# Attention outputs of heads 0 to 5: split into high and low parts at the store instead of at the reload

## The chip, the cores and the metric

The kernel runs on one core of one Trainium2 chip. The metric is the device time of one execution in microseconds. The core has five engines with a queue each, which wait for each other through semaphores: TensorE (PE in the rows, with its weight loads as PEld), VectorE (DVE), ScalarE (ACT), GpSimd (POOL) and SyncE (SP), which issues nearly all DMAs here. A queue is worked in order: an instruction that waits holds up all that stand behind it.

## The reference

One layer of a hybrid model over 1024 latent and 128 context tokens, width 1024: a half-step FFN, a token mixer, another half-step FFN, a final norm. The change lies in the mixer's attention and in the handing of its output to the up-projection:

```python
def mla_attention(q_nope, q_rope, k_nope, k_rope, v):   # 8 heads, dense softmax
    s = einsum('bqhd,bkhd->bhqk', qn, k_nope) + einsum('bqhr,bkr->bhqk', qr, k_rope)
    p = softmax(s * QK_SCALE)
    return einsum('bhqk,bkhd->bqhd', p, v)
...
merged = sigmoid(ga) * (o_attn @ w_up_attn) + sigmoid(gr) * (o_rec @ w_up_rec)
out = merged @ w_out
```

Latent queries attend to the 1024 latent keys and to 128 cached context keys; the context's 128 queries attend to the context alone.

## The kernel before

Everything is float32, and large matmuls are made of three: each operand is split into a high part (a cast to float32r, as TensorE takes it) and a low part (the operand less its high part), and high x high, high x low and low x high are summed in PSUM. So each operand of a large matmul costs a cast and a subtraction somewhere, on ScalarE, VectorE or GpSimd.

The stages follow each other: first FFN, the recurrent branch, attention (`attn`, `heads`), the merge of both branches (`merge`), second FFN. Activations lie with the features on the 128 partitions and the 1152 tokens (1024 latent, 128 context) along the row.

`heads` goes through the eight heads h, each in two blocks j of 512 queries; below, (h,j) is such a block. In `block`, nine steps over 128 keys each (t = 0 to 8) make the scores (three matmuls `sps`, L1620 to L1622), the exponential (ScalarE, `e`, L1624), its high part (ScalarE, `ehl`, L1627) and low part (GpSimd, or VectorE where t % 3 is 2, L1629). Two steps later `av` multiplies them with the values (three matmuls `po`, L1596 to L1598). Beside these steps, and woven between them, run:
- `rowmax` for a block to come: per block 12 matmuls `mps` (L1579), each followed by VectorE's maximum `mx` (L1580). They share two PSUM buffers with the projections, so TensorE can't run ahead of VectorE by more than two.
- in j = 0 of heads 1 to 6, `queries` of the next head: nine matmuls `qps` for each third of the tokens, and VectorE's subtraction and rotary products (L1560 to L1564);
- in j = 1, `keys` or `values` of the next pair of heads (heads 0 to 5), and `head_ctx`, the context queries of this head (output `pc`).
- in heads 6 and 7, `preload`, which fetches what the merge needs.

After the last step of a block, within the next block, `av` forms 1/sum on ScalarE (`rc`, L1604 and L1605) and the output `ob` (64 features x 512 queries) by three VectorE instructions (L1606 to L1608), and hands it to `put_oat`. A pair of heads makes one tile of 128 features, k = h // 2. For heads 0 to 5, `put_oat` stores the output as it is in DRAM (`oat`, one float32 array for each of the tiles 0 to 2), through SP. Heads 6 and 7 are split at once into the SBUF tiles `oh` and `ol` (L1472, L1473).

`preload` allocates `oh` and `ol` for seven tiles: 4 to 7 are the recurrent branch's, already stored in DRAM in two parts and loaded so (L1434); for 0 to 2 it loads a third of a row at a time into `oraw` (two buffers, L1440) and makes the high and low part on VectorE (L1441, L1443). Then it loads three tiles of up-projection weights and splits them (L1449, L1451). `heads` takes one step of `preload` after each step of a block, nine in a block, and a `yield` marks a step.

The order of each engine's queue is set by the framework's scheduler from the order of the code and its own estimates of durations; some instructions are pinned, none of those here. SP's queue holds stores, weight loads and `preload`'s loads in one row.

Of the kernel before, what the change touches and what calls it, by code (L numbers as in the profile page):

```python
# [9 lines left out]
F32 = mybir.dt.float32  # L10
F32R = mybir.dt.float32r
# [8 lines left out]
P = 128  # L20
D = 1024
KT = D // P
TL = 1024
TC = 128
T = TL + TC
TW = T + 8
CW = 384
NCH = T // CW
# [65 lines left out]
class Trunk:  # L94
# [630 lines left out]
    def mixer(self):  # L725
        nc, tc = self.nc, self.tc
        dram = lambda n, sh: self.dp.tile(sh, F32, name=n)
        self.sg = dram("sgates", [2, KT, P, T])
        self.orec = dram("orec", [4, 2, P, T])
        self.oat = dram("oat", [4, P, T])  # L730
        self.ahead = dram("ahead", [KT, P, REC[1] - REC[0]])
        self.wrec = dram("wrec", [KT // 2, 2, P, KT * P])
        with ExitStack() as st:
            self.fp = st.enter_context(tc.tile_pool(name="hp", bufs=1, reuse_waits="tile"))
            self.pp = st.enter_context(tc.tile_pool(name="pp", bufs=1, space=PSUM, reuse_waits="tile"))
            self.st, self.nt, self.hfb = ("sm", 3), ("t", 3), 2
            self.hgrn()
        with ExitStack() as st:
            self.kp = self.fp = st.enter_context(tc.tile_pool(name="kp", bufs=1, reuse_waits="tile"))
            self.pp = st.enter_context(tc.tile_pool(name="pp", bufs=1, space=PSUM, reuse_waits="tile"))  # L740
            self.attn()
# [686 lines left out]
    def preload(self):  # L1428
        nc = self.nc
        for k in (4, 5, 6, 7, 0, 1, 2):  # L1430
            th, tl = self.mo[k] = self.tt(F32R, "oh"), self.tt(F32R, "ol")
            if k > 3:
                for v, t in enumerate((th, tl)):
                    nc.sync.dma_start(t[:, :T].bitcast(F32), self.orec[k - 4, v])  # L1434
                yield
                continue
            for c in range(NCH):
                cs = slice(c * CW, (c + 1) * CW)
                raw = self.fp.tile([P, CW], F32, tag="vt", bufs=2, name="oraw")
                nc.sync.dma_start(raw, self.oat[k][:, cs])  # L1440
                nc.vector.tensor_copy(th[:, cs], raw)  # L1441
                yield
                nc.vector.tensor_sub(tl[:, cs], raw, th[:, cs])  # L1443
                yield
        self.ups = []
        for m in range(3):
            wh, wl, raw = self.load_up_all(m)
            self.ups.append((wh, wl))
            nc.scalar.copy(wh[:, :4], raw)  # L1449
            yield  # L1450
            nc.vector.tensor_sub(wl[:, :4], raw, wh[:, :4])  # L1451
            yield
# [8 lines left out]
            pin(nc.sync.dma_start(w[:, 4:8].rearrange("p k m -> p (k m)").bitcast(F32), src))  # L1461
        return wh, wl, raw

    def put_oat(self, h, r, cs, ob):
        nc = self.nc
        if h < 6:
            nc.sync.dma_start(self.oat[h // 2][r, cs], ob)
            return
        if self.mo[3] is None:
            self.mo[3] = self.tt(F32R, "oh"), self.tt(F32R, "ol")  # L1470
        th, tl = self.mo[3]
        nc.scalar.copy(th[r, cs], ob)  # L1472
        nc.vector.tensor_sub(tl[r, cs], ob, th[r, cs])  # L1473
# [116 lines left out]
    def av(self):  # L1590
        nc = self.nc
        h, j, t, po, V, eh, el = self.pend.pop(0)
        o = h % 2
        v = V[t // 3][:, t % 3].rearrange("p a d -> p (a d)")
# [11 lines left out]
        nc.vector.scalar_tensor_tensor(ob[A], po[B], -1.0, r[A], ALU.mult, ALU.mult)  # L1606
        nc.vector.tensor_mul(r[A], po[A], r[A])
        nc.vector.scalar_tensor_tensor(ob[A], ob[A], 2.0, r[A], ALU.add, ALU.mult)  # L1608
        self.put_oat(h, A, ts(j, 512), ob[A])

    def block(self, h, j, q, kt, V):
        nc = self.nc
# [22 lines left out]
    def head_ctx(self, h, qc, ktc, Vc):  # L1635
# [17 lines left out]
        po = self.pp.tile([64, P], F32, tag="tr", bufs=1, name="poc")  # L1653
        nc.tensor.matmul(po, Vc[:, r], Pt, start=True, stop=True)
        nc.scalar.copy(Pt[r], po)
        self.put_oat(h, r, slice(TL, T), Pt[r])
        yield

    def half(self, name, dt=F32):
# [823 lines left out]
```

## Time and profile before

| | us |
|---|---|
| three runs, median | 2806.1 |
| lowest and highest | 2804.52, 2806.98 |
| the profiled execution's own time | 2806.0 |
| its span, first to last instruction | 2804.2 |

The page gives busy time by engine. A busy TensorE is not TensorE at its peak, because matmuls overlap: one of 512 columns is shown with 0.39 us, and the next starts 0.23 us later. So holes are read better from the weight loads' idle time, with what ended it in brackets behind the row. Windows are stretches of the span; for each engine they give the busy time and, in parentheses, the number of its instructions, and at the end the granted TensorE clock, the DMA engines' busy share and GB/s. Attention's blocks lie between about 1540 and 1850 us of the span, and the granted clock is 1.00 in all of them.

### The profile page before, as it was taken

What the parts mean: (1) busy time and instruction counts of PE and PEld (TensorE: products, weight loads), DVE (VectorE), ACT (ScalarE), POOL (GpSimd) and SP (SyncE); (2) the same over time, 40 slices, a digit from 0 to 9 for tenths busy, and PEclk for the clock granted to TensorE, in tenths of its full rate; (3) what the DMA queues carried; (4) which work ended last, traced back from release to release, by engine and by line L of the source; (5) the groups of instructions that cost most, each with busy time, mean ns of one, the idle gap of its engine ahead of it and who ended that gap; (6) DMA issues with size and microseconds to landing.
All of it is one profiled execution on the core that took longest, in us unless ns stands there. A gap on an engine that the chain in (4) does not pass through costs nothing. (4 is left out here: it accounts for less than half of the span.)

```text
span 2804.2 us, 55762 instructions
## 1 busy us (share of the span) xinstructions
PE 2755.3 (98%) x21248; PEld 2633.2 (94%) x21248; DVE 2043.0 (73%) x4461; ACT 1299.5 (46%) x2695; POOL 922.9 (33%) x983
## 2 busy tenths in 40 slices
PE   9999999999999999999999999999999999999998
PEld 8999999999999998899998888689999999999997
DVE  8877777677778888887456777867666765568875
ACT  6532322322166677666436777741642322334332
POOL 0133223454221222222233444431414343423451
PEclk9999999999999999999999999999999999999999
DMA  6743333653121111212513001263454444357521
GB/s 260 228 132 120 124 127 125 242 203 110 58 94 59 44 61 41 66 45 85 187 63 102 19 14 29 86 242 122 144 174 132 156 141 137 113 170 249 163 85 68
DMA packets 219579, 337.66 MB, mean 120 GB/s; under 512 B 23664, under 2 KB 141360, under 8 KB 219312
## 3 DMA queue, kind: packets, MB, share of 16 engines
q1 hardware_dynamic: 218880, 333.96, 36.1%
q8 instruction: 168, 2.75, 0.4%
q14 instruction: 99, 0.81, 0.1%
q10 hardware_dynamic: 432, 0.14, 0.0%
HBM read 248.47 MB, written 85.54 MB: 119 GB/s over the span
## 5 line engine op out<-in xcount | busy, mean ns | idle before, releaser
L1933 PE MATMUL b<-xo,wo 128*128 128x288 f32 x3552 | 483.7, 295 | 1.1 <-DVE wo L1908 1.1
L1933 PEld LDWEIGHTS b<-xo,wo 128*128 128x128 f32 x3552 | 475.4, 188 | 1.3 <-DVE wo L1908 1.3
L1933 PE MATMUL b<-bh,wo 128*128 128x288 f32 x1776 | 366.2, 295 | 0.2 <-DVE hf L1866 0.2
L551 PE MATMUL mm<-xh,wh 128*128 128x384 f32 x928 | 323.7, 349 | 4.4 <-DVE sg L863 3.0
L553 PE MATMUL mm<-xh,wl 128*128 128x384 f32 x928 | 313.8, 338 | 0.0
L552 PE MATMUL mm<-xl,wh 128*128 128x384 f32 x928 | 313.1, 337 | 0.0
L1933 PEld LDWEIGHTS b<-bh,wo 128*128 128x128 f32 x1776 | 288.8, 188 | 0.4 <-ACT wo L1907 0.4
L581 DVE SCALAR_TENSOR_TENSOR x<-dn,modt,x 128x256 f32<-128x256 f32 (+4 forms) x472 | 225.4, 499 | 82.0 <-PE dn L553 79.8
L1933 PE MATMUL b<-bl,wo 128*128 128x288 f32 x888 | 261.9, 295 | 0.0
L1907 ACT CAST wo<-raw 128x512 fp32r<-128x512 f32 x185 | 114.7, 621 | 221.6 <-issue 90.4
L1908 DVE TENSOR_TENSOR wo<-raw,wo 128x512 fp32r<-128x512 f32 x185 | 127.6, 691 | 80.5 <-ACT wo L1907 78.0
L2134 PE MATMUL d<-xd,wd 128*128 128x288 f32 x1344 | 181.2, 296 | 5.0 <-DVE x L2121 3.5
L2134 PEld LDWEIGHTS d<-xd,wd 128*128 128x128 f32 x1344 | 178.5, 188 | 7.5 <-DVE x L2121 3.2
L551 PEld LDWEIGHTS mm<-xh,wh 128*128 128x128 f32 x928 | 174.7, 188 | 11.0 <-DVE sg L863 3.4
L552 PEld LDWEIGHTS mm<-xl,wh 128*128 128x128 f32 x928 | 175.0, 189 | 0.9
L553 PEld LDWEIGHTS mm<-xh,wl 128*128 128x128 f32 x928 | 174.9, 188 | 0.0
L1629 POOL TENSOR_TENSOR ehl<-e,ehl 128x512 fp32r<-128x512 f32 x93 | 122.0, 1315 | 150.9 <-ACT ehl L1627 78.2
L405 DVE SCALAR_TENSOR_TENSOR junk<-wada,cb 128x512 bf16<-128x512 f32 x224 | 164.1, 733 | 7.5 <-DMA wada<-in_w_aT 6.7
L1933 PEld LDWEIGHTS b<-bl,wo 128*128 128x128 f32 x888 | 167.4, 189 | 0.0
L1903 POOL TENSOR_TENSOR ws<-raw 128x256 f32<-128x256 f32 x74 | 66.0, 912 | 277.4 <-DMA raw<-in_w 200.2
L551 PE MATMUL ps<-bh,wh 128*128 128x288 f32 (+1 forms) x448 | 135.7, 303 | 1.3 <-DVE sl L1855 1.1
L1908 DVE TENSOR_TENSOR wo<-ws,wo 128x512 fp32r<-128x512 f32 x74 | 69.8, 943 | 87.7 <-ACT wo L1907 87.4
(478 smaller groups left out, 7172.1 us busy)
## 6 DMA issues: line engine op xcount, KB each, us to landing
raw<-in_w SPq DMA_DIRECT2D x148, 256.0 KB, 3.3
wada<-in_w_aT SPq DMA_DIRECT2D x112, 256.0 KB, 2.9
raw<-in_w SPq DMA_DIRECT2D x42, 512.0 KB, 4.1
raw<-in_w_in SPq DMA_DIRECT2D x41, 512.0 KB, 3.6
xr<-xd SPq DMA_DIRECT2D x56, 288.0 KB, 4.1
hr<-hs SPq DMA_DIRECT2D x26, 576.0 KB, 5.7
hb<-hd SPq DMA_DIRECT2D x44, 288.0 KB, 3.9
hs<-et SPq DMA_DIRECT2D x84, 144.0 KB, 2.3
```

Source lines behind the costliest of these rows:

```text
L405: nc.vector.scalar_tensor_tensor(junk, ws[n % 2], 1.0, cs[s], ALU.mult, ALU.mult, accum_out=o)
L551: pin(nc.tensor.matmul(ps, wh, xh, start=start and i == 0, stop=False))
L552: pin(nc.tensor.matmul(ps, wh, xl, start=False, stop=False))
L553: self.last_mm = nc.tensor.matmul(ps, wl, xh, start=False, stop=stop and i == n - 1)
L581: nc.vector.scalar_tensor_tensor(self.x[m][:, a:b], ps[:, a - lo : b - lo], self.modt[:, gm, m, s : s + 1], self.x[m][:, a:b], ALU.mult, A ...
L1629: eng.tensor_sub(el, e, eh)
L1903: nc.gpsimd.tensor_tensor(o[:, c], x[:, c], y[:, c], op)
L1907: nc.scalar.copy(wh, src[i])
L1908: nc.vector.tensor_sub(wl, src[i], wh)
L1933: nc.tensor.matmul(ps, w[:, k], x[:, k, :QW], start=first, stop=last, skip_group_check=home != i)
L2134: nc.tensor.matmul(ps, w[:, k], xv, start=start, stop=stop, skip_group_check=home != i)
```

## The change

For heads 0 to 5, the split is made where the output is formed, on VectorE, and both parts are stored: `oat` becomes two arrays for each tile. `preload` then loads `oh` and `ol` for tiles 0 to 2 with one DMA each and does nothing on VectorE; the number of its steps stays the same. The high part of `ob` goes into `rc`, which is free by then, and the low part into `ob` itself; the context output `pc` gets a small tile `pch` for its high part.

```diff
@@ mixer
-        self.oat = dram("oat", [4, P, T])
+        self.oat = dram("oat", [3, 2, P, T])
@@ preload
-            for c in range(NCH):
-                cs = slice(c * CW, (c + 1) * CW)
-                raw = self.fp.tile([P, CW], F32, tag="vt", bufs=2, name="oraw")
-                nc.sync.dma_start(raw, self.oat[k][:, cs])
-                nc.vector.tensor_copy(th[:, cs], raw)
-                yield
-                nc.vector.tensor_sub(tl[:, cs], raw, th[:, cs])
-                yield
+            for v, t in enumerate((th, tl)):
+                nc.sync.dma_start(t[:, :T].bitcast(F32), self.oat[k, v])
+                for _ in range(3):
+                    yield
@@ put_oat
-    def put_oat(self, h, r, cs, ob):
+    def put_oat(self, h, r, cs, ob, hi):
         nc = self.nc
         if h < 6:
-            nc.sync.dma_start(self.oat[h // 2][r, cs], ob)
+            nc.vector.tensor_copy(hi, ob)
+            lo = ob.bitcast(F32R)
+            nc.vector.tensor_sub(lo, ob, hi)
+            for v, t in enumerate((hi, lo)):
+                nc.sync.dma_start(self.oat[h // 2, v][r, cs], t.bitcast(F32))
             return
@@ av
-        self.put_oat(h, A, ts(j, 512), ob[A])
+        self.put_oat(h, A, ts(j, 512), ob[A], r[A].bitcast(F32R))
@@ head_ctx
-        self.put_oat(h, r, slice(TL, T), Pt[r])
+        hi = self.fp.tile([P, P], F32R, tag="pch", bufs=1, name="pch")
+        self.put_oat(h, r, slice(TL, T), Pt[r], hi[r])
```

The scheduler orders every queue anew from it. Outside attention the order of TensorE's matmuls stays as it was. Three places matter later. Each row below is a line of the code, an instruction, its output and inputs, and the output's size; line numbers of the changed kernel differ by up to four around `preload` and are the same from L1470 to L1655.

First, VectorE in block (6,1), from the store of the first output of head 6 on. Before:

```order
L1473 TENSOR_TENSOR ol<-ob,oh 64x512
L1441 CAST oh<-oraw 128x384
L1580 TENSOR_REDUCE mx_21306<-mps 128x1
L1443 TENSOR_TENSOR ol<-oraw,oh 128x384
L1580 TENSOR_REDUCE mx_21306<-mps 128x1 x3
L1441 CAST oh<-oraw 128x384
L1583 TENSOR_REDUCE m_21424<-mx_21306 128x4
L1629 TENSOR_TENSOR ehl<-e,ehl 128x512
L1443 TENSOR_TENSOR ol<-oraw,oh 128x384
L1441 CAST oh<-oraw 128x384
L1443 TENSOR_TENSOR ol<-oraw,oh 128x384
L1629 TENSOR_TENSOR ehl<-e,ehl 128x512
```

And of the changed kernel:

```order
L1473 TENSOR_TENSOR ol<-ob,oh 64x512
L1580 TENSOR_REDUCE mx_21357<-mps 128x1 x4
L1629 TENSOR_TENSOR ehl<-e,ehl 128x512
L1583 TENSOR_REDUCE m_21468<-mx_21357 128x4
L1629 TENSOR_TENSOR ehl<-e,ehl 128x512
```

The casts and subtractions of `oraw` are gone from between the row maxima and the exponentials' low parts.

Second, VectorE in block (2,0), behind the output of (1,1), whose last instruction is the first row. Before:

```order
L1608 SCALAR_TENSOR_TENSOR ob<-ob,rc 64x512
L1560 TENSOR_TENSOR ql_17932<-qps,qh_17931 64x256
L1562 TENSOR_TENSOR u<-qps,rope 32x256
L1563 TENSOR_TENSOR u<-qps,rope 32x256
L1580 TENSOR_REDUCE mx_19245<-mps 128x1
L1564 TENSOR_TENSOR u<-u 32x256
L1580 TENSOR_REDUCE mx_19245<-mps 128x1 x2
```

And of the changed kernel:

```order
L1608 SCALAR_TENSOR_TENSOR ob<-ob,rc 64x512
L1560 TENSOR_TENSOR ql_17932<-qps,qh_17931 64x256
L1463 CAST rc<-ob 64x512
L1562 TENSOR_TENSOR u<-qps,rope 32x256
L1465 TENSOR_TENSOR ob<-ob,rc 64x512
L1563 TENSOR_TENSOR u<-qps,rope 32x256
L1580 TENSOR_REDUCE mx_19262<-mps 128x1
L1564 TENSOR_TENSOR u<-u 32x256
L1580 TENSOR_REDUCE mx_19262<-mps 128x1 x2
```

The cast and the subtraction of the new split (L1463, L1465) stand ahead of three row maxima.

At the same place TensorE's queue, up to the first matmul of the second third of the query projection (`qps`). Before:

```order
L1598 MATMUL po<-ehl,V 128x512
L1620 MATMUL sps<-qh_17929,kth_17818 128x512
L1579 MATMUL mps<-kth_17818,qh_17929 128x384 x2
L1621 MATMUL sps<-qh_17929,ktl_17819 128x512
L1622 MATMUL sps<-ql_17930,kth_17818 128x512
L1596 MATMUL po<-ehl,V 128x512
L551 MATMUL qps<-qnh_17489,wh 128x384
```

And of the changed kernel:

```order
L1598 MATMUL po<-ehl,V 128x512
L1620 MATMUL sps<-qh_17929,kth_17818 128x512
L1621 MATMUL sps<-qh_17929,ktl_17819 128x512
L1622 MATMUL sps<-ql_17930,kth_17818 128x512
L1596 MATMUL po<-ehl,V 128x512
L1579 MATMUL mps<-kth_17818,qh_17929 128x384
L1597 MATMUL po<-ehl,V 128x512
L1579 MATMUL mps<-kth_17818,qh_17929 128x384
L1598 MATMUL po<-ehl,V 128x512
L1620 MATMUL sps<-qh_17929,kth_17818 128x512
L1621 MATMUL sps<-qh_17929,ktl_17819 128x512
L551 MATMUL qps<-qnh_17489,wh 128x384
```

The two `mps` moved behind three and four matmuls of 512 columns, and `qps` behind four more than before.

Third, SP's queue where `preload` begins with tile 0. Before:

```order
L1434 DMA ol<-orec 128x1152
L1440 DMA oraw<-oat 128x384 x2
L1467 DMA oat<-ob 64x512
L1440 DMA oraw<-oat 128x384 x7
L1458 DMA raw<-in_w_up 128x512
```

And of the changed kernel:

```order
L1434 DMA ol<-orec 128x1152
L1438 DMA oh<-oat 128x1152
L1467 DMA oat<-rc 64x512
L1467 DMA oat<-ob 64x512
L1438 DMA ol<-oat 128x1152
L1438 DMA oh<-oat 128x1152
L1438 DMA ol<-oat 128x1152
L1438 DMA oh<-oat 128x1152
L1438 DMA ol<-oat 128x1152
L1454 DMA raw<-in_w_up 128x512
```

Nine loads of thirds of a row became six of whole rows, and the last store of head 5 became two.

## The prediction

> **What bounds the kernel now.** I read first the shares of the whole span, then the windows of the attention blocks one by one, then TensorE's weight-load waits inside them, then what VectorE did there. The shares:
>
> ```profile
> PE 2755.3 (98%) x21248; PEld 2633.2 (94%) x21248; DVE 2043.0 (73%) x4461; ACT 1299.5 (46%) x2695; POOL 922.9 (33%) x983
> ```
>
> TensorE is the bound, so only its holes can be won or lost. The change touches the attention stage alone. A head h is worked in two blocks, j=0 and j=1; I write (h,j). I cut the stage where each block's closing logarithm (L1604) starts; the rows are, in order, (2,0), (2,1), (4,0), (6,0), (6,1), (7,0), (7,1), with window, length, and each engine's busy time:
>
> ```profile
> core 0: us, PE busy (x) PEld busy (x) DVE busy (x) ACT busy (x) POOL busy (x), PEclk, DMA share, GB/s
> ...
> 1603.80:1624.80 21.00, 20.94 (x100) 16.97 (x100) 17.46 (x33) 15.71 (x30) 11.34 (x10) 1.00 0.03 7
> 1624.80:1644.80 20.00, 19.97 (x98) 16.14 (x97) 13.94 (x29) 16.69 (x34) 8.60 (x8) 1.00 0.07 19
> ...
> 1686.50:1708.10 21.60, 21.06 (x100) 16.93 (x99) 18.35 (x33) 15.67 (x29) 10.91 (x10) 1.00 0.03 7
> ...
> 1769.80:1792.70 22.90, 20.74 (x98) 16.49 (x97) 21.02 (x37) 15.48 (x29) 11.29 (x9) 1.00 0.15 44
> 1792.70:1813.40 20.70, 16.96 (x76) 12.40 (x76) 19.35 (x32) 14.01 (x27) 9.59 (x8) 1.00 0.12 32
> 1813.40:1830.50 17.10, 16.19 (x73) 12.55 (x73) 15.25 (x25) 13.80 (x24) 7.03 (x6) 1.00 0.44 145
> 1830.50:1844.00 13.50, 12.56 (x51) 8.24 (x50) 8.83 (x15) 11.61 (x23) 2.59 (x2) 1.00 0.01 4
> ```
>
> In (2,0) to (4,0) TensorE is idle for 0.0 to 0.5 us of a block. In (6,0) and (6,1) it stands 2.2 and 3.7 us, and VectorE is busy 21.02 of 22.90 and 19.35 of 20.70: there VectorE paces. The waits of the weight loads show each hole (the bracket: idle time before it, and who ended it). First two of (2,0) and one of (4,0), then those over 0.6 us of (6,0), (6,1) and (7,0):
>
> ```profile
> 1610.37 0.47 PEld L1579 LDWEIGHTS mps<-kth,qh 96*128 96x128 f32 x2 [0.49 <-ACT qc L1557]
> 1611.69 0.19 PEld L551 LDWEIGHTS qps<-qnh,wh 128*128 128x128 f32 x1 [0.33 <-DVE mx L1580]
> ...
> 1701.80 0.30 PEld L1586 LDWEIGHTS mtr<-ident,m 128*1 128x1 f32 x4 [0.85 <-DVE m L1583]
> ...
> 1776.48 0.30 PEld L1579 LDWEIGHTS mps<-kth,qh 96*128 96x128 f32 x2 [0.90 <-DVE mx L1580]
> 1778.80 0.19 PEld L551 LDWEIGHTS qps<-qnh,wh 128*128 128x128 f32 x1 [1.21 <-DVE mx L1580]
> ...
> 1791.44 0.19 PEld L1579 LDWEIGHTS mps<-kth,qh 96*128 96x128 f32 x1 [1.08 <-DVE mx L1580]
> 1798.74 0.14 PEld L1650 LDWEIGHTS ptc<-ident,pc 128*128 128x128 f32 x1 [1.24 <-ACT oh L1472]
> 1802.05 0.19 PEld L1579 LDWEIGHTS mps<-kth,qh 96*128 96x128 f32 x1 [1.21 <-DVE mx L1580]
> 1806.21 0.19 PEld L1598 LDWEIGHTS po<-ehl,V 128*128 128x128 f32 x1 [1.08 <-DVE ehl L1629]
> 1812.71 0.19 PEld L1579 LDWEIGHTS mps<-kth,qh 96*128 96x128 f32 x1 [1.81 <-DVE mx L1580]
> 1819.68 0.19 PEld L1598 LDWEIGHTS po<-ehl,V 128*128 128x128 f32 x1 [1.10 <-DVE ehl L1629]
> 1822.00 0.19 PEld L1579 LDWEIGHTS mps<-kth,qh 96*128 96x128 f32 x1 [0.68 <-DVE mx L1580]
> ```
>
> **What goes: nine casts (L1441) and nine subtractions (L1443) in the last heads.** VectorE's own rows in (6,1), and the two groups with their count, busy time and mean:
>
> ```profile
> 1800.09 1.45 DVE L1441 CAST oh<-oraw 128x384 fp32r<-128x384 f32 x1
> ...
> 1801.92 0.54 DVE L1443 TENSOR_TENSOR ol<-oraw,oh 128x384 fp32r<-128x384 f32 x1
> ...
> 1804.12 0.35 DVE L1441 CAST oh<-oraw 128x384 fp32r<-128x384 f32 x1
> ...
> 1804.46 1.70 DVE L1629 TENSOR_TENSOR ehl<-e,ehl 128x512 fp32r<-128x512 f32 x1
> ...
> 1810.58 1.61 DVE L1443 TENSOR_TENSOR ol<-oraw,oh 128x384 fp32r<-128x384 f32 x1
> 1812.12 1.64 DVE L1580 TENSOR_REDUCE mx<-mps 128x1 f32<-128x384 f32 x3
> ```
> ```profile
> L1443 DVE TENSOR_TENSOR ol<-oraw,oh 128x384 fp32r<-128x384 f32 x9 | 8.2, 913 | 0.1
> L1441 DVE CAST oh<-oraw 128x384 fp32r<-128x384 f32 x9 | 5.2, 582 | 0.7 <-DMA oraw<-oat 0.6
> ```
>
> So 8.2 + 5.2 = 13.4 us of VectorE leave (6,0) to (7,0). What TensorE gets back:
> - (6,0) has the matmuls of (2,0) and (4,0) (98 to 100 records). Without the splits it falls to their lengths: 22.9 - 21.0 = 1.9, or 22.9 - 21.6 = 1.3. I take 1.9.
> - (6,1): the row maxima that TensorE waits for at 1802.05 and 1812.71 stand right behind the cast of 1.45 and the subtraction of 1.61 us: 1.21 + 1.81 = 3.0 go. The wait of 1.08 at 1806.21 stands behind a cast of 0.35, but also behind an exponential's own subtraction of 1.70 us; I take half. Sum 3.5, bounds 3.0 and 4.1. The 1.24 us at 1798.74 (a context probability) has no split ahead of it and stays; it is late next there.
> - (7,0): the two waits, 1.10 and 0.68, each have one split among several things ahead. 0 to 1.2; I take 0.5.
>
> Together **5.9 us gained, 4.3 to 7.2**. Where VectorE no longer paces (6,1), ScalarE with 14.0 us of work is next, and that is under the 20.7 - 3.5 = 17.2 left.
>
> **What comes: a cast and a subtraction behind each of twelve output blocks and six context outputs.** The subtraction is shown, clean, for both shapes (heads 6 and 7 are split so already):
>
> ```profile
> 1799.49 0.67 DVE L1473 TENSOR_TENSOR ol<-ob,oh 64x512 fp32r<-64x512 f32 x1
> ...
> 1809.26 0.28 DVE L1473 TENSOR_TENSOR ol<-pc,oh 64x128 fp32r<-64x128 f32 x1
> ```
>
> The row maxima of (2,0) that follow in VectorE's queue start here:
>
> ```profile
> 1610.04 0.56 DVE L1580 TENSOR_REDUCE mx<-mps 128x1 f32<-128x384 f32 x1
> ```
>
> A cast of 64x512 is not in the trace: at least 0.35 (the cast of 384 columns), at most 0.67 (the subtraction of 512); by columns 0.35 x 512/384 = 0.46, which I take. So 0.46 + 0.67 = 1.13 us per block, and 0.35 x 128/384 + 0.28 = 0.40 per context output: 12 x 1.13 + 6 x 0.40 = 16.0 us. VectorE's total work grows by 2.6 us; the change only moves it to blocks where TensorE paces. What of it TensorE feels:
> - The split of (h,0) runs in (h,1). There VectorE is busy 13.94 of 20.00, with 6 us free; I take 0.1 for each of six, bounds 0 and 0.25: 0.6.
> - The split of (h,1) runs in (h+1,0), six times, in front of the maxima at 1610.04 for which TensorE already waits. A price is in the trace: a product of 0.55 us (L1564) took 1.69 in (4,0), 1.14 more, and (4,0) is 21.6 - 21.0 = 0.6 us longer than (2,0), with a new wait of 0.85. So 0.6 is the upper end.
>
> ```profile
> 1616.53 0.55 DVE L1564 TENSOR_TENSOR u<-u 32x384 f32<-32x384 f32 x1
> ...
> 1699.27 1.69 DVE L1564 TENSOR_TENSOR u<-u 32x384 f32<-32x384 f32 x1
> ```
>
> The new order puts four more 512-column matmuls ahead of the query projection that waits there. Matmuls of that size follow each other each 0.23 us:
>
> ```profile
> 1800.19 0.39 PE L1597 MATMUL po<-ehl,V 128*128 128x512 f32 x1
> 1800.42 0.40 PE L1598 MATMUL po<-ehl,V 128*128 128x512 f32 x1
> ```
>
> So 0.93 us of other work covers 1.13: 0.2 is left, and six times that is 1.2, bounds 0 and 3.6. If this cover fails, it is the 0.6.
>
> **Transfers.** Eighteen stores become 36; SP, which issues them, does nothing else between blocks. Nine loads become six of 576 KB; five of them no longer wait for VectorE, but for buffers that the last query projection, in (6,0), frees. The issue of the up-projection weights that stands behind them on SP, the page's row of loads of that size (count, KB, us to landing), and a window in which many overlap (last number: GB/s):
>
> ```profile
> 1812.59 0.42 SPq L1458 DMA_DIRECT2D raw<-in_w_up  x1
> ```
> ```profile
> hr<-hs SPq DMA_DIRECT2D x26, 576.0 KB, 5.7
> ```
> ```profile
> 1850.00:1870.00 20.00, 20.00 (x153) 20.00 (x152) 11.21 (x26) 4.42 (x10) 8.53 (x10) 1.00 1.05 388
> ```
>
> Five loads are 2.95 MB, 7.6 us at 388 GB/s: from 1792.7, the end of (6,0), they land at 1800, and the weights behind them are issued some 20 us sooner than at 1812.59. One after the other they would take 5 x 5.7 = 29 us, to 1821: still ahead of the merge at 1844, but behind the opening of (7,0), where ScalarE now casts those weights with exponentials queued behind. I take 0, since the window shows that such loads overlap.
>
> **The sum.** -5.9 + 0.6 + 1.2 = **-4.1 us**. The profiled execution took 2806.0 us (span 2804.2), 0.1 under the median of three, 2806.1. So 2806.0 - 4.1 = **2801.9**. About 0.2%, 5.6 us, is what a measurement here can tell from no change: below 2800.5 counts as faster, above 2811.7 as slower.
>
> **Rivals.**
> - *Cover complete:* the order hides all splits, and the late heads give 5.9 to 7.2: about 2799.5. For: 6 us of free VectorE in j=1 blocks, the moved matmuls. Against: the waits that (2,0) has already.
> - *Collisions:* both new operations are of the kinds that sometimes take far longer here: L1443 means 913 ns against 540 clean, L1441 582 against 350, so 0.37 + 0.23 a block. Over twelve that is 7.2 us of VectorE; half falls in j=0 blocks, and 0.6/1.14 of that reaches TensorE: 1.9 us, so 2803.8. The 1.45 us cast at 1800.09 starts inside a GpSimd subtraction (a POOL row starts at 1799.97 and lasts 1.34), so it looks like a lock.
>
> ```profile
> 1799.97 1.34 POOL L1629 TENSOR_TENSOR ehl<-e,ehl 128x512 fp32r<-128x512 f32 x1 [1.42 <-PE sps L1622]
> ```
>
> The Trainium skill, "SBUF — State Buffer", section "Who interferes with whom", says that a cast, and a subtraction of two SBUF inputs, share ports with GpSimd and that the second to start blocks until the first is done; by that rule the trace agrees (1.45 against 0.35), and each split is exposed, which speaks against the change and for 2803.8 rather than 2801.9.
> - *Chain instead of VectorE:* in (6,1) the exponential, its cast and GpSimd's subtraction become the bound, as in (7,1), where TensorE stands 0.9 of 13.5 with VectorE at 8.83; then (6,1) and (7,0) give 1.0 instead of 4.0: -1.1, 2804.9.
> - *Slower:* the splits sit in VectorE's queue ahead of the row maxima whose two PSUM buffers TensorE needs, and all lands: 16.0 - 5.9 = +10.1, 2816.1. It loses from 0.5 us per block on (5.9/12). Against: (4,0) shows 0.6 in a j=0 block only, with no new order.
>
> **How the numbers follow.** Forecast 0.42, cover complete 0.25, collisions 0.20, chain 0.05, slower 0.08. The range reaches from the best gain with little cost (2806.0 - 7.2, and 0.9 for what runs of before differ: 2798.0) to a forecast whose costs are all at their bounds (2806.0 - 4.3 + 3.6 + 1.5 = 2806.8, 2807.0); it leaves out the slower case and the tail of the first. Faster: cover complete and a fifth of the forecast, 0.33; slower 0.08; same 0.59.
>
> **What would show it.** (6,1) near 17 us without waits of over 1 us for mx; (6,0) near 21; (1,0) to (5,0) longer by 0.2, with the wait before the second query projection still under 0.6. New L1463 and L1465 rows of over 1 us, or j=1 blocks longer than 20.0, would prove me wrong towards collisions or slower.

## The result and the profile after

| | before | after |
|---|---|---|
| time, median of 18 runs each | 2806.6 us (2804.3 to 2808.8) | 2811.3 us (2809.5 to 2813.5) |
| profiled execution, its span | 2806.0 us, 2804.2 us | 2813.5 us, 2811.4 us |

The ratio is 1.0019, 95% interval 1.0013 to 1.0026: the changed kernel is 4.7 us **slower**, where 4.1 us faster was forecast.

The shares of the whole span after the change (busy time, share, instructions of each engine):

```profile
PE 2757.1 (98%) x21248; PEld 2633.0 (94%) x21248; DVE 2053.5 (73%) x4479; ACT 1301.1 (46%) x2695; POOL 927.6 (33%) x983
```

VectorE is busy 10.5 us longer (2053.5 against 2043.0), where the working of the forecast had 2.6. The windows of single blocks after, cut as in the prediction, in order (0,1), (1,0), (1,1), (2,0), (2,1), then (6,0) to (7,1):

```profile
core 0: us, PE busy (x) PEld busy (x) DVE busy (x) ACT busy (x) POOL busy (x), PEclk, DMA share, GB/s
1542.50:1563.60 21.10, 20.23 (x98) 16.05 (x97) 16.31 (x33) 17.04 (x35) 9.15 (x7) 1.00 0.11 26
1563.60:1584.30 20.70, 20.26 (x98) 16.61 (x97) 17.71 (x33) 15.79 (x30) 12.06 (x11) 1.00 0.08 20
1584.30:1607.10 22.80, 21.75 (x107) 16.98 (x106) 15.13 (x29) 16.76 (x33) 9.25 (x8) 1.00 0.11 29
1607.10:1629.40 22.30, 20.94 (x99) 16.92 (x98) 19.40 (x35) 15.88 (x30) 11.14 (x10) 1.00 0.06 13
1629.40:1650.20 20.80, 20.45 (x99) 16.15 (x98) 15.88 (x33) 17.05 (x36) 9.90 (x8) 1.00 0.11 26
1780.50:1802.50 22.00, 20.77 (x99) 16.74 (x98) 18.90 (x34) 15.60 (x28) 10.50 (x9) 1.00 0.42 140
1802.50:1820.00 17.50, 16.49 (x77) 12.76 (x76) 12.52 (x25) 14.13 (x28) 8.02 (x7) 1.00 0.39 140
1820.00:1837.00 17.00, 15.85 (x70) 11.67 (x70) 13.14 (x21) 14.32 (x26) 8.40 (x6) 1.00 0.15 47
1837.00:1849.90 12.90, 12.48 (x52) 8.66 (x51) 8.31 (x13) 11.05 (x23) 2.80 (x3) 1.00 0.00 0
```

(6,1) fell from 20.7 to 17.5, as forecast, and (2,1), a j=1 block in which VectorE is still idle for 4.9 us, grew from 20.0 to 20.8. All lengths, to 0.01 us between the starts of the closing logarithms of two blocks, in one table; "L1465" is the duration of the new subtraction in that block:

| block | (0,1) | (1,0) | (1,1) | (2,0) | (2,1) | (3,0) | (3,1) | (4,0) | (4,1) | (5,0) | (5,1) | (6,0) | (6,1) | (7,0) | (7,1) |
|---|---|---|---|---|---|---|---|---|---|---|---|---|---|---|---|
| before | 20.01 | 20.72 | 20.92 | 21.02 | 20.01 | 20.76 | 20.93 | 21.64 | 19.99 | 20.75 | 20.92 | 22.84 | 20.79 | 17.08 | 13.51 |
| after minus before | +1.08 | 0.00 | +1.92 | +1.28 | +0.73 | -0.04 | +1.97 | +0.66 | +0.81 | -0.06 | +1.95 | -0.76 | -3.31 | -0.07 | -0.61 |
| L1465 | 1.78 | 0.68 | 1.78 | 1.33 | 1.20 | 0.68 | 1.81 | 1.33 | 1.20 | 0.68 | 1.80 | 1.41 | | | |

The last four blocks win 4.75 us, the eleven before them lose 10.30, of which the six j=1 blocks 8.46. That is +5.6, against +4.7 between the medians and +7.2 between the two profiled spans: the rest of the 7.2 lies before and behind these blocks, and the profiled execution of the changed kernel was the slowest of its 18.

The third row sorts the blocks. Where the subtraction took 0.68 us, the block kept its length, though it had 1.1 us more of VectorE; where it took 1.2 to 1.8, the block grew ((6,0) against what it should have won, as the next section shows). What happens in (1,1): VectorE's and GpSimd's rows, then TensorE's weight load that waits (start, duration, engine, line, operation, tiles):

```profile
1589.64 0.42 DVE L1463 CAST rc<-ob 64x512 fp32r<-64x512 f32 x1
1590.10 0.56 DVE L1580 TENSOR_REDUCE mx<-mps 128x1 f32<-128x384 f32 x1
1590.68 1.78 DVE L1465 TENSOR_TENSOR ob<-ob,rc 64x512 fp32r<-64x512 f32 x1
1592.50 0.56 DVE L1580 TENSOR_REDUCE mx<-mps 128x1 f32<-128x384 f32 x1
```
```profile
1590.63 1.29 POOL L1629 TENSOR_TENSOR ehl<-e,ehl 128x512 fp32r<-128x512 f32 x1 [4.53 <-ACT ehl L1627]
```
```profile
1593.11 0.19 PEld L1579 LDWEIGHTS mps<-kth,qh 96*128 96x128 f32 x1 [1.47 <-DVE mx L1580]
```

GpSimd's subtraction begins at 1590.63, VectorE's 0.05 us later. GpSimd's ends at 1591.92, VectorE's 0.54 us behind that. This holds in all nine blocks in which the subtraction is long: GpSimd's row began 0.03 to 0.90 us before it, and VectorE's ended 0.55 us after GpSimd's each time, to 0.01 us, for the 0.68 that it takes alone. So its length is what is left of GpSimd's row, and 0.55. The next row maximum stands behind it in the queue and begins at 1592.50, and TensorE, out of PSUM buffers for scores, has stood still 1.47 us. In (1,0) the order of the two is the other way round:

```profile
1568.99 0.68 DVE L1465 TENSOR_TENSOR ob<-ob,rc 64x512 fp32r<-64x512 f32 x1
1569.70 0.43 DVE L1563 TENSOR_TENSOR u<-qps,rope 32x256 f32<-32x256 f32 x1
1570.16 0.56 DVE L1580 TENSOR_REDUCE mx<-mps 128x1 f32<-128x384 f32 x1
1570.75 0.42 DVE L1564 TENSOR_TENSOR u<-u 32x256 f32<-32x256 f32 x1
```
```profile
1569.16 3.16 POOL L1629 TENSOR_TENSOR ehl<-e,ehl 128x512 fp32r<-128x512 f32 x2 [4.10 <-PE sps L1622]
```

VectorE began at 1568.99, GpSimd 0.17 later; VectorE is clean and GpSimd's two rows take 3.16 us together (a single one has a median of 1.29 in the trace of before). And the sum L1564 behind it, here a clean 0.42 us, was stretched at this place before the change:

```profile
1568.00 1.06 DVE L1564 TENSOR_TENSOR u<-u 32x256 f32<-32x256 f32 x1
```

So (1,0) paid for a part of its 1.1 us of new work with stretching that went away: 0.64 us here, 0.37 over the whole block, since a later L1564 in it is now stretched by 0.28. Blocks of one kind repeat this to 0.03 us: 1.78, 1.81, 1.80 in (1,1), (3,1), (5,1).

So the theory was: **stretching** (the "collision theory" of the expectations: the second to start of two operations with two SBUF inputs, one on VectorE and one on GpSimd, waits for the first), in front of the row maxima, whose delay TensorE then feels. Its rivals: plain **work** (1.1 us in front of the maxima costs, stretched or not), and **order** (the scheduler's new order of TensorE and ScalarE costs). In the runs below, "blocks" is the sum of (0,1) to (5,1) minus before, "late" that of (6,0) to (7,1); times and ratios are against runs of the kernel before on the same chip, with 95% intervals.

### The profile page after: what moved, and what is told of

The parts are those of the page before. It is cut to its first block, busy times and chain, and to the rows that moved or that the text cites. A ratio compares the mean times of both kernels' runs of the same rounds, so it can differ in the third digit from the quotient of the medians.

```text
span 2811.4 us, 55837 instructions
## 1 busy us (share of the span) xinstructions
PE 2757.1 (98%) x21248; PEld 2633.0 (94%) x21248; DVE 2053.5 (73%) x4479; ACT 1301.1 (46%) x2695; POOL 927.6 (33%) x983
```

## The gain alone and the cost alone

```diff
-            nc.vector.tensor_copy(hi, ob)
-            lo = ob.bitcast(F32R)
-            nc.vector.tensor_sub(lo, ob, hi)
-            for v, t in enumerate((hi, lo)):
-                nc.sync.dma_start(self.oat[h // 2, v][r, cs], t.bitcast(F32))
+            for v in range(2):
+                nc.sync.dma_start(self.oat[h // 2, v][r, cs], ob)
```

> The gain alone: heads 0 to 5 store the unsplit output twice, with no cast and no subtraction, and the last heads load the two parts as in the changed kernel; this leaves the split of heads 0 to 5 out. All theories: (0,1) to (5,1) as long as before the change, (6,0) to (7,1) shorter by about 4.7 us together as in the changed kernel, 2801.5 to 2802.5. If the late heads gain less than that here, part of the 4.7 came from elsewhere.

Measured: 2799.6 us against 2805.3, ratio 0.9980 (0.9972 to 0.9989). Late -5.83: (6,0) -1.72, (6,1) -3.42, (7,0) -0.06, (7,1) -0.63. The other blocks are within 0.03 of before, but for (4,0), -0.63, where an L1564 of 1.69 us took 0.55. The windows of (6,0) and (6,1):

```profile
1769.79:1790.91 21.12, 20.65 (x101) 16.89 (x99) 16.97 (x32) 15.45 (x29) 10.70 (x9) 1.00 0.49 166
1790.91:1808.28 17.37, 16.37 (x76) 12.64 (x75) 12.39 (x25) 14.06 (x27) 7.76 (x6) 1.00 0.35 122
```

The time is 1.9 us under what was expected. The 5.9 us of the forecast are there, and 1.1 more than the changed kernel shows, since its last split still runs in (6,0). This kernel makes all the new stores and loads, so the transfers cost nothing that shows. The split is what costs. It was then put alone into the kernel before:

```diff
 # kernel before
         if h < 6:
+            nc.vector.tensor_copy(hi, ob)
+            nc.vector.tensor_sub(hi, ob, hi)
             nc.sync.dma_start(self.oat[h // 2][r, cs], ob)
```

> The cost alone: the kernel before with the cast and the subtraction of the split added on VectorE behind each output of heads 0 to 5 (their result is stored nowhere), the unsplit output stored and the last heads loading and splitting as before. Collision theory: subtractions of over 1 us in most blocks, and 8 to 11 us more than before, 2814 to 2818; blocks where the subtraction takes 0.7 keep their length. Work theory: the same total, but blocks with a clean subtraction grow too. If it is under 2810, the transfers or the two stores of the changed kernel had a part in the cost.

Measured: 2814.9 against 2805.3, ratio 1.0036 (1.0023 to 1.0048). Blocks +9.72, of which j=1 8.40, each block within 0.07 us of the changed kernel's but for (5,0), 0.32 shorter. (1,0), (3,0) and (5,0), with a subtraction of 0.68, did not grow, as the first theory had it and the second had not. So the cost in these blocks is that of the split on VectorE, with one store or two, whatever the last heads do. (The last four blocks were 1.8 us longer than before here, (7,0) by 4.1 and (6,1) 2.3 shorter; why stays open.)

## Taking the stretching away

First the same operands in another instruction:

```diff
-            nc.vector.tensor_sub(lo, ob, hi)
+            nc.vector.scalar_tensor_tensor(lo, ob, 1.0, hi, ALU.mult, ALU.subtract)
```

> The changed kernel with one edit: the subtraction of the split (L1465) is written as scalar_tensor_tensor (ob*1.0 - hi), same operands, same result, same place in every engine's order. Collision theory (the new subtraction, 0.68 us clean, is locked out by a GpSimd subtraction in nine of twelve blocks and takes 1.20 to 1.81 us, and the row maxima behind it come late): scalar_tensor_tensor on the same two tiles (L1608) was never stretched, so L1465 takes about 0.68 in all twelve, (0,1) to (5,1) fall back towards their old lengths, and the time falls by 7.5 us (the sum of the stretching) to 10.4 us (the sum by which those blocks grew): 2801 to 2804. Work theory (1.1 us more on VectorE in front of the row maxima is what costs, stretched or not): at least half of the 10.4 stays, 2806 to 2809. Order theory (TensorE's and ScalarE's new order costs it): no change, 2811.

Measured: 2810.3, ratio 1.0018 (1.0009 to 1.0027); blocks +10.16. The time is the one named for the order theory, but the run puts no theory to the test, since the stretching was still there:

```profile
L1465 DVE SCALAR_TENSOR_TENSOR ob<-ob,rc x12: 683/1330/1801, 1549.6 to 1787.9; 64x512 fp32r<-64x512 f32 x12
```

The columns are minimum, median and maximum in ns. The expectation rested on L1608, the same kind of operation, which was never stretched in the kernel before (0.67 to 0.69 us in 16 rows). That was luck of its place, not of its kind: in the changed kernel one of its 16 rows, in (7,0), took 1.67. What has to go is the second SBUF input:

```diff
-            nc.vector.tensor_sub(lo, ob, hi)
+            nc.vector.tensor_reduce(lo[:, 0:1], hi, AX.X, ALU.max)
```

> The changed kernel with the subtraction (L1465) replaced by a row maximum over the same 64x512 high part, an operation with one SBUF input; every engine keeps the order of the changed kernel instruction by instruction. The low part is left out (it holds the unsplit output). Collision theory: no row of L1465 over 0.8 us whatever GpSimd does beside it, (0,1) to (5,1) fall from 10.4 us over their old lengths to 0 to 3, time 2801 to 2804. Work theory (any 0.7 us there costs): at least 7 of the 10.4 stay, 2808 to 2811. Order theory: all of it stays, 2811.

Measured: 2807.2 against 2807.2, ratio 0.9999 (0.9990 to 1.0008), every queue keeps the order of the changed kernel, and the row is clean in all twelve:

```profile
L1465 DVE TENSOR_REDUCE ob<-rc x12: 666/675/684, 1547.4 to 1782.3; 64x1 fp32r<-64x512 f32 x12
```

In (1,1) the pair met as in the changed kernel, GpSimd 0.04 us ahead, and where TensorE had waited 1.47 us it now waits 0.37:

```profile
1589.88 0.68 DVE L1465 TENSOR_REDUCE ob<-rc 64x1 fp32r<-64x512 f32 x1
```
```profile
1589.84 1.28 POOL L1629 TENSOR_TENSOR ehl<-e,ehl 128x512 fp32r<-128x512 f32 x1 [4.53 <-ACT ehl L1627]
```
```profile
1591.21 0.19 PEld L1579 LDWEIGHTS mps<-kth,qh 96*128 96x128 f32 x1 [0.37 <-DVE mx L1580]
```

In the j=1 blocks this is the cleanest number of the study. There L1465 was stretched by 5.49 us in the changed kernel (1.78 + 1.78 + 1.20 + 1.81 + 1.20 + 1.80 less six times 0.68), and 8.46 - 5.49 = 2.97. With no stretching and the same order, the j=1 blocks cost 2.96: there **the stretching reaches TensorE one for one**. It holds block by block, too: from (0,1) to (5,1) the growth less the stretching is -0.02, 0.82, 0.21, 0.84, 0.29 and 0.83, and this run measures -0.06, 0.81, 0.26, 0.83, 0.33 and 0.79. But all blocks together still cost 6.78, where the first theory expected 0 to 3 and 2801 to 2804 us, and the work theory 2808 to 2811: the time lies between the two. The j=0 blocks got worse, from +1.84 to +3.82: (1,0), (3,0), (5,0) went from 0 to +0.9. Here is (1,0):

```profile
1567.21 0.68 DVE L1465 TENSOR_REDUCE ob<-rc 64x1 fp32r<-64x512 f32 x1
1567.92 0.43 DVE L1563 TENSOR_TENSOR u<-qps,rope 32x256 f32<-32x256 f32 x1
1568.38 0.56 DVE L1580 TENSOR_REDUCE mx<-mps 128x1 f32<-128x384 f32 x1
1568.97 1.39 DVE L1564 TENSOR_TENSOR u<-u 32x256 f32<-32x256 f32 x1
```
```profile
1568.79 1.29 POOL L1629 TENSOR_TENSOR ehl<-e,ehl 128x512 fp32r<-128x512 f32 x1
```

Where the split had two SBUF inputs and came first, it held GpSimd back, and L1564 found GpSimd's next operation out of its way. Now GpSimd begins 0.18 us before L1564, and L1564 waits for it: 1.39 - 0.42 = 0.97 us, and the block is 0.97 longer. The stretching had moved to the next candidate. Two ways take it from the split with its full result kept (in both, and in the one on GpSimd behind them, the scheduler orders the queues anew), first by PSUM:

```diff
-        nc.vector.scalar_tensor_tensor(ob[A], ob[A], 2.0, r[A], ALU.add, ALU.mult)
+        fin = po[A] if h < 6 else ob[A]
+        nc.vector.scalar_tensor_tensor(fin, ob[A], 2.0, r[A], ALU.add, ALU.mult)
...
+        # put_oat: hi = cast of fin, lo (SBUF) = fin (PSUM) - hi
```

> The changed kernel with the last product (L1608) of heads 0 to 5 written to the PSUM tile po instead of SBUF, so that the cast and the subtraction of the split have one PSUM and one SBUF input; the result is the same. Collision theory: L1465 about 0.7 us in all twelve blocks; the cast may take 0.7 instead of 0.42 and the PSUM buffer comes free 1 us later; 2801 to 2806. Work theory: VectorE's clean work is as much or more (1.1 to 1.4 us a block), so 2809 to 2812.

Measured: 2808.4 against 2807.2, ratio 1.0003 (0.9994 to 1.0012). The j=1 blocks fell to +2.74, the j=0 blocks rose to +5.29, with L1564 stretched by 0.7 to 1.1 us in each; the cast from PSUM took 0.69. Then by ScalarE, which moves the subtraction to another time:

```diff
-            nc.vector.tensor_copy(hi, ob)
+            nc.scalar.copy(hi, ob)
...
-            nc.vector.tensor_sub(lo, ob, hi)
+            nc.vector.scalar_tensor_tensor(lo, ob, 1.0, hi, ALU.mult, ALU.subtract)
```

> The changed kernel with the cast on ScalarE and the subtraction as scalar_tensor_tensor: VectorE does 0.68 us a block instead of 1.1 clean. Collision theory: as with scalar_tensor_tensor alone, or up to 1 us better, 2800 to 2804; ScalarE has 0.45 us more in blocks where it is busy 14 to 16 of 20 us, which may cost 0 to 0.2 a block. Work theory: better than scalar_tensor_tensor alone by 2 us or more. Order theory: nothing can be said, since the order differs here.

Measured: 2805.4 against 2805.3, ratio 1.0000 (0.9991 to 1.0009). L1465 took 0.68 to 0.69 in all twelve, being the first to start each time, and the j=1 blocks cost 1.20; the j=0 blocks cost 4.02, with 1.6 to 1.85 us of stretching in the three L1564 of each. Two of them in (1,0), the smaller form first:

```profile
1568.45 1.40 DVE L1564 TENSOR_TENSOR u<-u 32x256 f32<-32x256 f32 x1
1575.78 1.29 DVE L1564 TENSOR_TENSOR u<-u 32x384 f32<-32x384 f32 x1
```

Both times were over what the first theory expected, and the stretching of L1564 is the likely reason; the first is also only 0.6 us under what the work theory had. And the subtraction on GpSimd itself:

```diff
-            nc.vector.tensor_sub(lo, ob, hi)
+            nc.gpsimd.tensor_sub(lo, ob, hi)
```

> The changed kernel with the subtraction of the split on GpSimd, the cast on VectorE; the result is the same. Collision theory: VectorE's row maxima are not held up by the split itself, but GpSimd has about 1.3 us more in front of its exponentials' low parts, and VectorE's other two-input operations meet it: cost of 0 to 6 us, 2800 to 2806. Work theory: as with the cast alone plus GpSimd's delay, 2803 to 2809.

Measured: 2816.7 against 2807.2, ratio 1.0033 (1.0021 to 1.0046), worse than any theory said. One such subtraction takes GpSimd 1.29 us, and (3,0) and (5,0) grew by 3.1 and 3.2, with one L1564 of 2.61 us in each. The engine that is the other party of the stretching is no refuge.

## The other candidate

L1564 can lose its second SBUF input too, if the second product of the rotation stays in the PSUM tile that it reads:

```diff
-                nc.vector.tensor_mul(u[R, 1], ps[96:P, v], rope[96:P, lo:hi])
-                nc.vector.tensor_add(u[R, 0], u[R, 0], u[R, 1])
+                nc.vector.tensor_mul(ps[R, v], ps[96:P, v], rope[96:P, lo:hi])
+                nc.vector.tensor_add(u[R, 0], u[R, 0], ps[R, v])
```

In the kernel before:

> The kernel before with only L1563 written to PSUM (control). Collision theory: L1564 was stretched there by 0.23 to 1.15 us in (1,0) to (5,0), and only the 1.15 of (4,0) was seen to cost 0.6: 2803.5 to 2806, and (4,0) as long as (2,0). Work or order theory: no change, 2806.5.

Measured: 2803.6 against 2805.3, ratio 0.9991 (0.9982 to 0.9999). L1564 before, and now:

```profile
L1564 DVE TENSOR_TENSOR u<-u x24: 416/550/1694, 1491.5 to 1789.1; 32x384 f32<-32x384 f32 x16, 32x256 f32<-32x256 f32 x8
```
```profile
L1564 DVE TENSOR_TENSOR u<-u,qps x24: 419/552/554, 1490.3 to 1787.1; 32x384 f32<-32x384 f32 x16, 32x256 f32<-32x256 f32 x8
```

The median is the same, the maximum is gone, and (4,0) is 0.37 us shorter, now as long as (2,0) (21.27 and 21.29), which itself grew by 0.27. The scheduler's order changed with the edit, and 1.6 of the 2.0 us that these blocks won lie in the last four, where no L1564 had been stretched: so the 1.7 us are not shown to be L1564's. The same edit beside the three ways of the split:

> The changed kernel with the row maximum in place of the subtraction (as in the run before with it, the low part is left out), and with the second product of the query rotation (L1563) written to the PSUM tile it reads, so that the sum behind it (L1564) has one SBUF input. Collision theory (each two-input operation of VectorE that meets a GpSimd one is stretched, and when the split no longer is, L1564 is: 1.24 to 1.54 us more in (1,0), (3,0), (5,0)): no L1564 row over 0.7 us, (1,0), (3,0) and (5,0) fall by 0.9 each, the even j=0 blocks by 0.2, so 3 to 4.5 us less than with L1564 as it was: 2803 to 2804.5, and what then stays of the cost in (0,1) to (5,1), 2.5 to 4 us, is the clean work of the split. Work or order theory: L1564 had no part, and the time stays at 2807.

> The changed kernel with the cast of the split on ScalarE, its subtraction as scalar_tensor_tensor, and L1563 written to PSUM; the result is the same. Collision theory: with the cast on ScalarE no split was stretched, but L1564 was by 1.6 to 1.85 us in each j=0 block, and these blocks were 0.5 to 1.1 us longer; with L1564 clean they are within 0.3 of before: 2800.5 to 2803. ScalarE theory (its 0.61 us cast holds up exponentials in j=0 blocks): no change, 2805.

> The changed kernel with the last product (L1608) of heads 0 to 5 in PSUM, and L1563 written to PSUM: neither the split nor L1564 has two SBUF inputs, all on VectorE, same result. Collision theory: j=0 blocks, 0.6 to 1.6 us longer than before with L1564 stretched by 0.7 to 1.1, fall to 0 to 0.5; 2803 to 2805.5. Work theory: no change, 2808.

Measured: 2811.1 (ratio 1.0017, 1.0009 to 1.0026), 2806.9 (1.0006, 0.9997 to 1.0016) and 2805.6 (1.0001, 0.9992 to 1.0010): two misses, and the third at the edge of what was expected. The order is another one in all three. No L1564 was stretched in any of them, and yet the eleven blocks together cost 9.67, 5.19 and 6.99 us, where they had cost 6.78, 5.21 and 8.03 without this edit. In the first the *cast* now met GpSimd:

```profile
L1463 DVE CAST rc<-ob x12: 407/424/1478, 1548.1 to 1786.1; 64x512 fp32r<-64x512 f32 x12
```

By 1.07 in (1,1) and (3,1) and by 0.63 in (2,1) and (4,1), which cost 1.7 and 1.3. In the second, the split's subtraction was again stretched by 1.02, 1.05 and 1.12 in (2,0), (4,0) and (6,0). In the third nothing of the split was, but one exponential's subtraction (L1630 there) by 1.1 in (0,1), and (5,1) was 5.0 us longer and (5,0) 2.5 shorter: work moved across the cut, which left 87 and 116 matmuls in them for 97 and 106 in the run with PSUM alone. In the first two another pair met once the queues had shifted. That the j=0 blocks pay for L1564's stretching is therefore shown where the order was kept, with the row maximum ((1,0), (3,0) and (5,0) 0.97, 0.95 and 0.95 us longer than in the changed kernel for 0.97, 0.96 and 0.96 of stretching), and not confirmed by these three.

## Work or order: what is left

```diff
-            nc.vector.tensor_sub(lo, ob, hi)
```

> The changed kernel without the subtraction: the cast alone is on VectorE and the unsplit output is stored as the low part; this leaves the low part out. Collision theory: the cast was never stretched (0.41 to 0.43), so blocks (0,1) to (5,1) cost 0 to 1.5 us together and the time is 2799.5 to 2801.5. Work theory: 0.42 of 1.1 us of work stays, so about 4 us of cost: 2803 to 2805. The order of TensorE and ScalarE is a different one here, so up to 2 us may be put down to it.

Measured: 2802.2 against 2807.2, ratio 0.9983 (0.9975 to 0.9992); blocks +1.79, of which (1,1), (3,1), (5,1) +0.54 to +0.58 each, with no cast stretched. The 2.96 us of the unstretched j=1 blocks were then cut down step by step, with the order kept in the first step:

```diff
-            nc.vector.tensor_sub(lo, ob, hi)
+            nc.vector.memset(ob.bitcast(BF16)[:, : ob.shape[-1]], 0.0)
```

> The changed kernel with the subtraction (L1465) replaced by a fill of the low part's first 256 words (the low part is left out); every engine keeps the order of the changed kernel instruction by instruction, and the fill has no SBUF input and should take about 0.27 us (a fill of 128x256 took 0.272 elsewhere in the kernel) where the row maximum took 0.68 and the subtraction 0.68 to 1.81. If what is left of the cost without stretching is clean work in VectorE's queue, the blocks that had no stretching with the row maximum fall by about the 0.41 that is taken out, (1,1), (3,1), (5,1) from +0.8 to +0.4 and (2,1), (4,1) from +0.3 to 0, 2.5 to 4 us less than with the row maximum in sum: 2802.5 to 2805. If it is the new order of TensorE and ScalarE, (1,1), (3,1) and (5,1) stay at +0.8 and the time at 2806 to 2807.

```diff
             if ob.shape[-1] == 512:
-                nc.vector.tensor_copy(hi, ob)
+                nc.vector.memset(hi.bitcast(BF16)[:, :224], 0.0)
 # beside the edit above
```

> As the run with the fill in place of the subtraction, with the cast (L1463) of the twelve output blocks replaced by a fill of the high part's first 112 words; the split of these blocks is left out, and VectorE does about 0.4 us a block in its place. TensorE's order in (2,0), (3,1), (4,0) and (4,1) is that of the changed kernel, matmul by matmul; in (1,1) and (5,1) a few matmuls stand elsewhere. If what was left in (3,1) with the single fill (+0.66 over before) is clean VectorE work, it falls by about the 0.3 that is taken out, to 0.2 to 0.4, and (2,0), where the cast and L1564 stood in front of the maxima, from +0.87 to 0.3 to 0.6. If it is the new order of TensorE, (3,1) stays at 0.6 to 0.7 and (2,0) at 0.8 to 0.9. Time 2801 to 2803.5 in the first case, 2803.5 to 2804.5 in the second.

Measured: 2804.0 against 2805.2 (ratio 0.9995, 0.9986 to 1.0004) and 2802.7 against 2805.6 (0.9989, 0.9979 to 0.9998). The two fills took 0.27 and 0.15 us. With the single fill every queue has the order of the changed kernel. With two fills it has not, and not only where the expectation says so: in the trace of each j=1 block, (3,1) and (4,1) too, one or two `mps` stand one or two places elsewhere among the matmuls, and VectorE works the second fill ahead of a row maximum that stood before it. By block, with the work of the split in it:

| | work, us | (2,0) | (1,1) | (3,1) | (5,1) | (2,1) | (4,1) | all j=1 |
|---|---|---|---|---|---|---|---|---|
| changed kernel | 1.6 to 2.2 | +1.28 | +1.92 | +1.97 | +1.95 | +0.73 | +0.81 | 8.46 |
| row maximum | 1.09 | +0.80 | +0.81 | +0.83 | +0.79 | +0.26 | +0.33 | 2.96 |
| cast and fill | 0.69 | +0.87 | +0.63 | +0.66 | +0.62 | +0.29 | +0.29 | 2.45 |
| two fills | 0.42 | +0.85 | +0.37 | +0.45 | +0.35 | +0.30 | +0.28 | 1.74 |

The context output's own cast and subtraction in each j=1 block (0.22 and 0.29 us, with the fills 0.22 and 0.11) are not in the column "work". (2,1) and (4,1) do not move with the work at all: there, +0.3 is left when 0.67 of 1.09 us of it is gone, and in the kernel with the cast alone, whose order is another one, they are at 0.00. That speaks for order, in that place. In (1,1), (3,1) and (5,1), with the order kept, 0.17 of 0.8 goes with the first 0.41 us of work, where the work case had 0.4; another 0.2 to 0.27 goes with two fills, where work and order changed together. The last run falls between its two cases: (3,1) at +0.45 and the time speak for work, (2,0) at +0.85 for the other, though there the sum of the rotation (L1564) is stretched by 0.8 in its turn. So of the 2.96 us 0.51 went with the work alone and 0.71 with work and order; what the 1.74 that is left is made of stays open. It shows as TensorE waiting ahead of the row maxima's matmuls: in (1,1) the weight loads' waits of over 0.3 us before `mps` add up to 2.15 us in the changed kernel, 1.05 with the row maximum, 0.68 with one fill and 0.34 with two, and there is none in the kernel before; the block grew by 1.92, 0.81, 0.63 and 0.37.

## Looking for a version without the cost

If the gain hangs on taking the split of the last heads off VectorE there, and not on where else it is done, it can go to other engines in place. Both kernels are the one before with L1563 in PSUM:

```diff
-                nc.vector.tensor_copy(th[:, cs], raw)
+                nc.scalar.copy(th[:, cs], raw)
 # second kernel, beside it
-                nc.vector.tensor_sub(tl[:, cs], raw, th[:, cs])
+                nc.gpsimd.tensor_sub(tl[:, cs], raw, th[:, cs])
```

> The kernel before with L1563 written to PSUM and the nine casts of the last heads on ScalarE; the split stays where it was, in the last heads. If late-head VectorE work and its stretching are what the change wins back, most of it is to be had so: 5.2 us of casts leave VectorE, (6,0) and (6,1) fall by 2 to 4 us together against the 0.3 to 3.6 that L1563 in PSUM alone left, and the time is 2800.5 to 2802.5, under both kernels. If ScalarE's casts hold up exponentials there, nothing is won: 2803 to 2805.

> As the run with the casts on ScalarE, with the nine subtractions on GpSimd: nothing of the split of heads 0 to 5 is on VectorE anywhere. If VectorE's work in the last heads is the cost, (6,0) to (7,0) are as short as in the gain alone: 2799.5 to 2801.5. If GpSimd's subtractions (about 1 us each) hold up its own exponentials' low parts or stretch VectorE's two-input operations, 2802 to 2805.

Measured: 2803.4 against 2805.2, ratio 0.9993 (0.9984 to 1.0002), and 2802.8, ratio 0.9989 (0.9980 to 0.9998). The second is 2.4 us faster than the kernel before, and so faster than the changed kernel. But with L1563 in PSUM alone it was 1.7 us (ratio 0.9982 to 0.9999), and the intervals overlap: that moving the split adds to it is not shown. Each came out in the less good of its two cases: late is -1.0 and -2.6, for -1.6 with L1563 alone and -5.8 with the gain alone, and (6,1) falls by 1.7 and 1.2 us, not 3.4. The traces show stretching that goes on there. In the first, the subtractions that stayed on VectorE take twice their clean 0.55 us in the median:

```profile
L1443 DVE TENSOR_TENSOR ol<-oraw,oh x9: 551/1182/1645, 1782.5 to 1818.7; 128x384 fp32r<-128x384 f32 x9
```

In the second, VectorE's own low parts of exponentials take 1.45, 1.43 and 0.99 in (6,0) and (6,1), for 0.69. How much of the missing gain that explains was not measured.

## Why the prediction was wrong, point by point

- **The gain of 5.9 us**: right as a sum, for (6,0) and (6,1) by its mechanism. The gain alone measured 5.83 in the last four blocks: (6,0) 1.72 of 1.9, (6,1) 3.42 of 3.5, (7,0) 0.06 of 0.5, and 0.63 in (7,1), which no term had; that the last two cancel is luck. The wait of 1.24 us for a context probability stayed, as said:

```profile
1808.35 0.14 PEld L1650 LDWEIGHTS ptc<-ident,pc 128*128 128x128 f32 x1 [1.24 <-ACT oh L1472]
```

- **The new operations**: cast 0.42 for the 0.46 taken, subtraction clean 0.68 for 0.67; per context output 0.22 + 0.29 = 0.51 for 0.40. Clean, these were near.
- **The failed step**: "The split of (h,0) runs in (h,1). There VectorE is busy 13.94 of 20.00, with 6 us free; I take 0.1 for each of six, bounds 0 and 0.25: 0.6." Measured: 8.46 us, 1.4 a block: 5.49 of stretching, which the term had at nothing, and 2.97 that stay without it. Free time of an engine in a block is an average over 20 us. The row maxima, 0.56 us each, stand before, between and behind the two new operations, with two PSUM buffers for their scores, so TensorE waits for whatever stands ahead of the next maximum, however idle VectorE is in the rest of the block. The windows show it: (1,1) has VectorE busy 15.13 of 22.80, and TensorE waits all the same. The forecast is off by 8.8 us (-4.1 against +4.7), this term alone by 7.9.
- **The collisions** were seen, and put as a rival at 1.9 us with a chance of 0.20. The mechanism was right, and so was the sum of the stretching: 7.2 us of VectorE worked out, 7.5 measured in L1465. The parts were not: the means over past rows gave 0.37 us to each subtraction and 0.23 to each cast, where nine of twelve subtractions were stretched by 0.5 to 1.1 us and no cast, so that the sum fits is in part luck. What failed is the share that TensorE feels: the half in j=1 blocks was put at nothing, without a reason, and the other at 0.6/1.14. The runs show that in j=1 blocks all 5.49 us are felt.
- **j=0 blocks**, 0.2 each under the cover of the moved matmuls: near in (1,0), (3,0), (5,0), 0.0, but with the help of 0.1 to 0.4 us of stretching of L1564 that went away, and no run tests the cover by itself; wrong in (2,0), (4,0) and (6,0), where L1465 took 1.33 to 1.41. (6,0) gave 0.96 us of its gain back (1.72 against 0.76).
- **Transfers**, 0: right, as far as the gain alone shows no cost with all of them in it. The weights' issue moved from 1812.59 to 1799.54, by 13 us where about 20 was worked out:

```profile
1799.54 0.38 SPq L1454 DMA_DIRECT2D raw<-in_w_up  x1
```

- **The slower rival** had the place right (the split ahead of the row maxima and their two buffers) and breaks even at 0.5 us a block. Measured, the eleven blocks (0,1) to (5,1) lost 0.94 each on average. The evidence brought against it, that (4,0) showed 0.6 in a j=0 block only, was one collision of the kernel before, in whose j=1 blocks no row was stretched: it could say nothing of what one would cost there.
- Of what would show it, "rows of over 1 us" came true for L1465 and not for L1463. "j=1 blocks longer than 20.0" was no sign at all: it was read off (2,1), and (1,1), (3,1) and (5,1) took 20.9 us before the change. (6,1) came to 17.5 as said, (6,0) to 22.1 for "near 21".

On the rule behind this, the Trainium skill, "SBUF — State Buffer", section "Who interferes with whom", says that a VectorE operation with two SBUF inputs contends with a GpSimd one that reads SBUF and that the second to issue blocks in full, whatever its kind. The runs agree: 1.78 us when GpSimd was 0.05 ahead, 0.68 when VectorE was 0.17 ahead and GpSimd paid; with one SBUF input 0.684 at most in twelve of twelve; "in full" is 0.55 of 0.68 us after GpSimd's end. The forecast cited the rule, gave it a chance of 0.20, and let a quarter of its delay reach TensorE.

## What to carry to other kernels

An operation added to a busy queue is not priced by the engine's free time in a stage, but by what stands next behind it and how many buffers that has: list the two or three rows behind the new one and the consumer that waits for them. Where two engines hold each other up, a mean over past collisions can give the sum, but not where it falls: look up, at the very place, which row of the other engine is running, and price two cases, nothing if the new operation starts first, and the rest of the other's row if it starts second. Then ask who waits behind it. Taking one collision away can move the queues so that another pair meets, so look at that before counting the gain.

## What the runs showed that was not expected

- A few hundredths of a microsecond decide. In the kernel before, L1564 began 0.02 us before GpSimd's row in (2,0) and took 0.55 us; in (4,0) it began 0.01 us after it and took 1.69. The two rows of GpSimd:

```profile
1616.55 1.69 POOL L1629 TENSOR_TENSOR ehl<-e,ehl 128x512 fp32r<-128x512 f32 x1 [3.55 <-issue]
```
```profile
1699.26 1.29 POOL L1629 TENSOR_TENSOR ehl<-e,ehl 128x512 fp32r<-128x512 f32 x1 [3.53 <-issue]
```

- A VectorE operation with two SBUF inputs can shield others by holding GpSimd back: with the row maximum in its place, L1564 in (1,0) took 1.39 us instead of 0.42.
- scalar_tensor_tensor on two SBUF tiles is stretched like the subtraction (1.80 for 1.81 us in one place), and a cast from SBUF to SBUF is too, at times (1.48 for 0.42 us).
- Operations with one PSUM and one SBUF input were not: L1564 went from a maximum of 1.69 us to 0.55 over 24 rows, with its median unchanged.
